# A passage between two projections, ordered by hand: from the output projection to gate/up in a two-layer trunk on one core

## The chip, the core and the metric

The kernel runs on one core of a Trainium2 chip, whose engines work side by side: TensorE (PE; its weight loads are shown apart as PEld), VectorE (DVE), ScalarE (ACT), GpSimd (POOL) and SyncE (SP), which issues most DMAs. The metric is the device time of one launch in microseconds (us), smaller is better; of several runs the median counts.

## What is computed

The reference is a trunk of two layers over 256 tokens of width 2048, all in float32. Around the change it does this:

```python
x = x + rms_norm(mix @ w_o, post_mix_norm[l])     # 2048 -> 2048
h = rms_norm(x, pre_ffn_norm[l])
f = (silu(h @ w_gate) * (h @ w_up)) @ w_down      # 2048 -> 5632 -> 2048
x = x + rms_norm(f, post_ffn_norm[l])
```

Here `mix` is the joined result of two kinds of attention. The passage meant by the change is the end of `mix @ w_o`, the norm and the sum into `x`, the transposition of the new `x`, and the first products with `w_gate` and `w_up`. It occurs once in each layer, so twice in a run.

## The kernel before

**Split products.** Every float32 product is made of three products of rounded numbers: a weight is split into a rounded part `hi` and a rest `lo`, the activations likewise into a rounded part and a rest, and PE adds hi x hi, hi x lo and lo x hi into one PSUM bank. A weight tile holds two blocks of 128 rows by 512 columns (128x1024 on the chip). ACT rounds it (L307, `hi`), DVE forms the rest (L317, `lo`). Some sums of a pair of weights are shared by Strassen's seven products (`seven_products`), which is not touched. In a few chosen places of gate/up the rest is made on GpSimd instead (L310).

**The stream of weights.** All weights lie in one list in the order of use. `fetch` issues their DMAs on SP ahead of time (four `raw` buffers), `feed` makes `hi` and `lo` (six buffers each) for the next one, and `weights(i, ahead)` feeds up to `ahead` further. Call the first of the last four `w_o` tiles `idx`: `idx`..`idx+3` are those four, `idx+4`/`idx+5` are gate and up for the first pair of blocks of x columns (pair 0), `idx+6`/`idx+7` for pair 1, `idx+8`/`idx+9` for pair 3, which comes third in the order of use, `idx+10`/`idx+11` for pair 2. A buffer of `hi` and `lo` comes free six weights later, so `idx+10` waits for the last use of `idx+4`.

**The tokens.** They form two tiles of 128, t0 and t1. The 2048 columns form four groups (cg0 to cg3) of 512, each with four blocks of 128.

**The end of the output projection.** Columns 2 and 3 of the projection are summed in four PSUM banks (two groups by two token tiles). The last four weights, 24 products for t0 and then 24 for t1, are issued so that t0 ends first. As each group ends, `evac_sum` adds the part shared by Strassen's products (L589), has ACT square it for the norm (L591 or L586) and multiplies by the gain (L592 or L587). `rescale` takes the root of the mean square: three small DVE operations (L599 to L601), Ln and Exp on ACT (L602, L603), one more on DVE (L604), a Newton step in two (L476, L477), and then four operations x = m * r + x, one per column group (L627).

**The transposition.** `transposed` turns one column group of x with four PE transposes into a bank of PSUM (tag `acc`, four banks), ACT rounds the four blocks with the next norm's gains (L488), and DVE makes the four rests (L493). The results are the stationary operands (`xF`) of gate/up.

**Gate/up.** `eight` (L1250) makes twelve products for one pair of blocks and one token tile. The first chunk takes pairs 0 and 1 for t0 and then for t1, and after them pairs 3, 2, 7 and so on for both tiles. Pairs 0 and 1 need cg0, pairs 3 and 2 need cg1, the others cg2 and cg3. The factor of the norm itself (`inv_rms`, eight squares L512 on ACT) is needed only at the end of a chunk.

**The order.** A list scheduler of the library fixes each engine's order ahead of the run, by priority (place in the program, or earlier by an offset under `high_priority`) and by its own estimate of when things are ready. Each engine then issues in that order and waits where an operand is late. In a `manual_schedule` region the named engines keep the order of the program among the region's instructions; where these fall among other instructions of that engine stays with the scheduler. Before the change such a region covers ACT and DVE from the last four `w_o` weights to the transposition of t0. The end of t1 (`evac_sum` of its last group, `rescale`, its transposes) stands outside under high priority.

Of the kernel before, what the change touches and what calls it, by code (L numbers as in the profile page):

```python
# [9 lines left out]
F32 = mybir.dt.float32  # L10
F32R = mybir.dt.float32r
BF16 = mybir.dt.bfloat16
AF = mybir.ActivationFunctionType
ALU = mybir.AluOpType
# [153 lines left out]
def kernel(  # L168
# [152 lines left out]

    rests = []
# [156 lines left out]

    def transposed(t, g0, tiles, cols=range(4)):  # L480
        for cg in cols:
            pb = acc_bank(f"xT_ps{t}_{cg}")
            for j in range(4):
                k = cg * 4 + j
                nc.tensor.transpose(pb[:, j * P : (j + 1) * P], x_part(t, k * P, P), ident)
            for j in range(4):
                k = cg * 4 + j
                rounded = nc.scalar.activation(  # L488
                    tiles[k][:, 0, t * P : (t + 1) * P], pb[:, j * P : (j + 1) * P], AF.Copy, scale=gains[:, g0 + k : g0 + k + 1]
                )  # L490
            for j in range(4):
                k = cg * 4 + j
                rest = nc.vector.scalar_tensor_tensor(  # L493
                    out=tiles[k][:, 1, t * P : (t + 1) * P],
                    in0=pb[:, j * P : (j + 1) * P],
                    scalar=gains[:, g0 + k : g0 + k + 1],
                    in1=tiles[k][:, 0, t * P : (t + 1) * P].bitcast(F32),
                    op0=ALU.mult,
                    op1=ALU.subtract,
                )  # L500
        return rounded, rest
# [4 lines left out]
    def inv_rms(t, pool, nm, parts=None):  # L506
        ss = small.tile([P, 1], F32, tag="ssx", name=f"ssx_{nm}_{t}")
        part = small.tile([P, 4], F32, tag="ssp", name=f"ssp_{nm}_{t}")
        for h in range(4):
            if parts is None:  # L510
                junk = pool.tile([P, CW], F32, tag="t2", name=f"junk_{nm}_{t}_{h}")
                nc.scalar.activation(junk, x_part(t, h * CW, CW), AF.Square, accum_out=part[:, h : h + 1])  # L512
            else:
                nc.scalar.activation(parts[h], parts[h], AF.Square, accum_out=part[:, h : h + 1])
# [66 lines left out]

    def evac_sum(pool, acc, mg, ssm, gpost, c, t, nm, summed=False):
        m = mg[t, c // 2][:, c % 2, :]
        if summed:
            junk = pool.tile([P, CW], F32, tag="t2", name=f"jm_{nm}_{t}_{c}")
            nc.scalar.activation(junk, acc, AF.Square, accum_out=ssm[t][:, c : c + 1])  # L586
            nc.vector.tensor_tensor(out=m, in0=acc, in1=gpost[:, c * CW : (c + 1) * CW], op=ALU.mult)  # L587
            return
        nc.vector.tensor_tensor(out=m, in0=acc, in1=m, op=shared_sign(t, c % 2))  # L589
        junk = pool.tile([P, CW], F32, tag="t2", name=f"jm_{nm}_{t}_{c}")  # L590
        nc.scalar.activation(junk, m, AF.Square, accum_out=ssm[t][:, c : c + 1])  # L591
        nc.vector.tensor_tensor(out=m, in0=m, in1=gpost[:, c * CW : (c + 1) * CW], op=ALU.mult)  # L592

    def rescale(mg, ssm, t, nm, then=None, newest=None):
        halves = newest is not None
# [5 lines left out]
        nc.vector.tensor_scalar(out=half, in0=three, scalar1=-0.5 / D, scalar2=-0.5 * EPS, op0=ALU.mult, op1=ALU.add)  # L601
        nc.scalar.activation(u, fourth, AF.Ln, scale=1.0 / D, bias=most)  # L602
        nc.scalar.activation(r, u, AF.Exp, scale=-0.5)  # L603
        nc.vector.tensor_scalar(out=ms, in0=fourth, scalar1=-0.5 / D, scalar2=half, op0=ALU.mult, op1=ALU.add)  # L604
        newton(r, u, ms)
        if halves:
# [8 lines left out]
        for c in range(4):  # L615
            if halves and c == 0:
                continue
            if halves and c == 3:
# [7 lines left out]
            sl = x_part(t, c * CW, CW)  # L626
            nc.vector.scalar_tensor_tensor(  # L627
                out=sl, in0=mg[t, c // 2][:, c % 2, :], scalar=r, in1=sl, op0=ALU.mult, op1=ALU.add
            )
# [505 lines left out]
    for l in range(L):  # L1135
# [48 lines left out]
        with tc.manual_schedule(engines={mybir.EngineType.Activation, mybir.EngineType.DVE}):  # L1184
            feed(idx + 6)
            for n, (c, kp) in enumerate(last_o):
                unit({0: accs[c, 0]}, mix, idx + n, kp, (0,), False, kp == LAST_O[-1], 0)
                if kp == LAST_O[-1]:
                    evac_sum(pool, accs[c, 0], mg, ssm, gpost, c, 0, f"o{l}")
            rescale(mg, ssm, 0, f"o{l}")  # L1190
            for n, (c, kp) in enumerate(last_o):
                feed(idx + 7 + n)
                fetch(min(idx + 12 + n, idx + 12))
                unit({1: accs[c, 1]}, mix, idx + n, kp, (1,), False, kp == LAST_O[-1], 0)
                transposed(0, 32 + l * KT, xT, cols=(n,))
                if (c, kp) == (2, LAST_O[-1]):
                    evac_sum(pool, accs[2, 1], mg, ssm, gpost, 2, 1, f"o{l}", True)
        with tc.high_priority(offset=URGENT):
            evac_sum(pool, accs[3, 1], mg, ssm, gpost, 3, 1, f"o{l}", True)
            rescale(mg, ssm, 1, f"o{l}", lambda t, c: transposed(t, 32 + l * KT, xT, cols=(c,)))  # L1200
        open_sums[0] = False
        rs = [inv_rms(t, pool, f"ffn{l}") for t in range(NT)]
# [272 lines left out]
```

## Time and profile before

| what | us |
|---|---|
| median of 3 runs | 2181.57 |
| lowest, highest | 2181.53, 2182.70 |
| profiled execution, whole | 2183.48 |
| its span, first to last instruction | 2181.7 |
| PE busy in the span | 2166.0 |
| DVE busy | 1920.7 |
| ACT busy | 1400.4 |
| POOL busy | 260.5 |

The profile is of one execution. Times in its views count from the start of the span. A row of the timeline gives the start, the duration, the engine, the line of the kernel, the operation, output and inputs, and how many like ones follow each other; in square brackets stands how long the engine was idle before and what released it. Products are pipelined: each is shown with 0.39 us, while the next starts after 0.23 us. In the view by windows each engine has its busy time and, in brackets, the number of its instructions.

### The profile page before, as it was taken

The numbers are of one execution on the slowest core, as the hardware profiler recorded it, in microseconds if no ns is written. First come the engines' busy times: TensorE is split into PE (matmuls) and PEld (weight loads), VectorE is DVE, ScalarE is ACT, GpSimd is POOL, SyncE is SP. The second block draws the span as 40 slices with busy tenths as digits, with TensorE's granted clock in tenths as the row PEclk, the third lists the DMA queues.
The fourth block names the chain that finished last, engine by engine and source line by source line (L and its number), as shares of the span: only waits on it lengthen the run. The fifth ranks groups of instructions, "written<-read, shape, count | busy, mean of one in ns | idle before, by whom it ended". The sixth has DMA issues, their size and how long they took to land.

```text
span 2181.7 us, 28784 instructions
## 1 busy us (share of the span) xinstructions
PE 2166.0 (99%) x9944; PEld 1781.7 (82%) x9944; DVE 1920.7 (88%) x2657; ACT 1400.4 (64%) x2089; POOL 260.5 (12%) x243
## 2 busy tenths in 40 slices
PE   9999999999999999999999999999999999999998
PEld 7888888788888888888878888887888888888886
DVE  7888658899999999999878886589999999999997
ACT  7666665756666656666665666657666666576664
POOL 1100000031222221000010000000212222200000
PEclk9999999999999999999999999999999999999999
DMA  9544555488887767767465555555888877768683
GB/s 323 194 164 174 193 184 176 165 300 234 239 258 229 226 231 233 239 223 258 149 241 174 172 174 188 191 164 191 286 237 241 262 222 227 240 225 244 204 268 100
DMA packets 140851, 471.49 MB, mean 216 GB/s; under 512 B 16016, under 2 KB 17040, under 8 KB 140192
## 3 DMA queue, kind: packets, MB, share of 16 engines
q1 hardware_dynamic: 121952, 436.03, 57.7%
q0 software_dynamic: 18176, 33.07, 9.2%
q8 instruction: 78, 1.28, 0.2%
q14 instruction: 69, 0.57, 0.1%
q10 hardware_dynamic: 576, 0.54, 0.1%
HBM read 461.19 MB, written 8.39 MB: 215 GB/s over the span
## 4 chain that ended last, share of the span: by engine, by line
PE 94%; DVE 3%; ACT 2%; issue 1%; DMA 0%; SPq 0%; DVEq 0%; ACTq 0%
PE c L1250 19%; PE in L1084 7%; PE in L1086 7%; PE in L1085 7%; PE dn L1357 4%; PE dn L1356 4%; PE dn L1359 4%; PE p L1085 3%; PE c L1084 3%; PE p L1084 3%; PE p L1086 3%; PE c L1085 3%; PE c L1086 3%; PE o L569 2%; PE o L571 2%; PE o L570 2%
## 5 line engine op out<-in xcount | busy, mean ns | idle before, releaser
L317 DVE TENSOR_TENSOR lo<-raw,hi 128x1024 fp32r<-128x1024 f32 x468 | 561.9, 1220 | 103.3 <-ACT hi L307 102.3
L307 ACT ACTIVATE hi<-raw 128x1024 fp32r<-128x1024 f32 x490 | 501.5, 1053 | 102.3 <-DMA raw<-in_weights_in_turn_dram 41.8
L1250 PE MATMUL c<-hi,xF 128*128 128x512 f32 x1280 | 345.9, 391 | 1.5 <-DVE xF L493 1.5
L1250 PEld LDWEIGHTS c<-hi,xF 128*128 128x128 f32 x1280 | 238.3, 188 | 50.3 <-DVE xF L493 2.0
L258 POOL DMA_DIRECT2D T<-in_weights_in_turn_dram x126 | 111.2, 883 | 1373.8 <-DMA T<-in_weights_in_turn_dram 716.6
L1250 PE MATMUL c<-lo,xF 128*128 128x512 f32 x640 | 198.2, 390 | 2.5 <-DVE lo L317 2.5
L279 ACT ACTIVATE Th<-G 128x1024 fp32r<-128x1024 f32 x126 | 133.1, 1056 | 79.8 <-DVE G L291 78.6
L281 DVE TENSOR_TENSOR Tl<-G,Th 128x1024 fp32r<-128x1024 f32 x126 | 153.9, 1221 | 10.1 <-ACT Th L279 10.1
L1356 PE MATMUL dn<-hi,jh 128*128 128x512 f32 x416 | 162.0, 389 | 0.0
L1357 PE MATMUL dn<-lo,jh 128*128 128x512 f32 x416 | 161.8, 389 | 0.0
L307 ACT ACTIVATE hi<-G 128x1024 fp32r<-128x1024 f32 x126 | 132.9, 1055 | 44.6 <-DMA G<-in_weights_in_turn_dram 27.8
L281 DVE TENSOR_TENSOR lo<-T,hi 128x1024 fp32r<-128x1024 f32 x126 | 159.6, 1266 | 0.3 <-ACT hi L279 0.2
L279 ACT ACTIVATE Th<-T 128x512 fp32r<-128x512 f32 x126 | 79.7, 633 | 118.6 <-DVE T L290 113.3
L291 DVE TENSOR_TENSOR G<-G,T 128x1024 f32<-128x1024 f32 x126 | 153.5, 1218 | 1.8
L1250 PEld LDWEIGHTS c<-lo,xF 128*128 128x128 f32 x640 | 120.1, 188 | 28.1 <-DVE lo L317 3.0
L317 DVE TENSOR_TENSOR lo<-G,hi 128x1024 fp32r<-128x1024 f32 x108 | 131.6, 1219 | 12.3 <-ACT hi L307 12.2
L279 ACT ACTIVATE hi<-T 128x1024 fp32r<-128x1024 f32 x126 | 132.2, 1049 | 12.1 <-PE c L1086 10.6
L1084 PE MATMUL in<-hi,xT 128*128 128x512 f32 x328 | 131.0, 401 | 0.6 <-DVE xT L862 0.6
L1084 PE MATMUL in<-hi,xI 128*128 128x512 f32 x328 | 131.1, 401 | 0.0
L1085 PE MATMUL in<-lo,xI 128*128 128x512 f32 x328 | 128.0, 390 | 0.3 <-DVE lo L317 0.3
L1085 PE MATMUL in<-lo,xT 128*128 128x512 f32 x328 | 127.8, 391 | 0.4 <-DVE lo L891 0.4
L1359 PE MATMUL dn<-hi,jl 128*128 128x512 f32 x416 | 128.0, 389 | 0.0
(485 smaller groups left out, 4954.2 us busy)
## 6 DMA issues: line engine op xcount, KB each, us to landing
raw<-in_weights_in_turn_dram SPq DMA_DIRECT2D x490, 512.0 KB, 4.6
T<-in_weights_in_turn_dram SPq DMA_DIRECT2D x126, 512.0 KB, 5.3
G<-in_weights_in_turn_dram SPq DMA_DIRECT2D x126, 512.0 KB, 5.4
T<-in_weights_in_turn_dram POOLq DMA_DIRECT2D x126, 256.0 KB, 6.1
GU<-in_weights_in_turn_dram SPq DMA_DIRECT2D x32, 512.0 KB, 6.5
V<-in_weights_in_turn_dram SPq DMA_DIRECT2D x8, 512.0 KB, 3.7
away_ffn<-x SPq DMA_DIRECT2D x8, 512.0 KB, 8.2
xd<-away_ffn SPq DMA_DIRECT2D x8, 512.0 KB, 9.4
```

Source lines behind the costliest of these rows:

```text
L279: nc.scalar.activation(h, w, AF.Copy)
L281: newest_rest[i] = nc.vector.tensor_tensor(out=l, in0=w, in1=h.bitcast(F32), op=ALU.subtract)
L291: nc.vector.tensor_tensor(out=g, in0=g, in1=t2.unsqueeze(1).to_broadcast([P, 2, CW]), op=ALU.add)
L307: nc.scalar.activation(hi, raw, AF.Copy)
L317: rest = nc.vector.tensor_tensor(out=lo, in0=raw, in1=hi.bitcast(F32), op=ALU.subtract)
L1084: nc.tensor.matmul(a, sh, hi, start=first, stop=False, skip_group_check=open_sums[0])
L1085: nc.tensor.matmul(a, sh, lo, start=False, stop=False, skip_group_check=open_sums[0])
L1086: return nc.tensor.matmul(a, sl, hi, start=False, stop=last, skip_group_check=open_sums[0])
L1250: nc.tensor.matmul(a, stat[part], w[j][:, kk, :], start=first and kk + n == 0, stop=last and kk == 1 and n == 2)
L1356: nc.tensor.matmul(accs[c, t], sh, hi[:, kk, :], start=first, stop=False, skip_group_check=open_sums[0])
L1357: nc.tensor.matmul(accs[c, t], sh, lo[:, kk, :], start=False, stop=False, skip_group_check=open_sums[0])
L1359: nc.tensor.matmul(accs[c, t], sl, hi[:, kk, :], start=False, stop=last, skip_group_check=open_sums[0])
```

## The change

One region now covers ACT, DVE and PE from the last four `w_o` weights on, and a second one, under high priority, covers ACT and DVE for the rest of the passage.

- `idx+5` is split behind the square of t0's group 2, and not ahead of the sum that this square reads.
- All 48 last products of the output projection stand ahead of t0's sixteen transposes on PE; all four groups of t0 are turned at once into the four `acc` banks.
- Of t0 only cg0 and cg1 are rounded and get rests before t1's turn; cg2 and cg3 come behind t1's cg0 and cg1.
- The rest of `idx+7` (up, pair 1) is made on GpSimd, behind the rest of `idx+6`, to which it has a dependence.
- The root for t1 is interleaved by hand with the splits of `idx+8` and `idx+9`, the gains of t1's groups 2 and 3 come behind the first two sums into x.
- The eight squares of `inv_rms` are issued on ACT behind the rounding of t1's cg0 (`turned`).

The same functions are cut into smaller ones (`turned_x`, `rounded_x`, `rest_of_x`, `squared`, `gained`, `shared_added`, `root_of`, `rescaled`); the operations in them are the same. `rounded_next` issues the rounding of the next weight and gives back a function that makes its rest. The core of the diff:

```diff
+    def rounded_next():
+        i = fed[0]
+        fetch(i + 1)
+        raw = raws[i]
+        hi = wpool.tile([P, 2, CW], F32R, tag="hi", bufs=6, name=f"hi{i}")
+        nc.scalar.activation(hi, raw, AF.Copy)
+        lo = wpool.tile([P, 2, CW], F32R, tag="lo", bufs=6, name=f"lo{i}")
...
+        def rest(eng=nc.vector):
+            r = eng.tensor_tensor(out=lo, in0=raw, in1=hi.bitcast(F32), op=ALU.subtract)
...
-        with tc.manual_schedule(engines={mybir.EngineType.Activation, mybir.EngineType.DVE}):
-            feed(idx + 6)
+        by_hand = {mybir.EngineType.Activation, mybir.EngineType.DVE}
+        with tc.manual_schedule(engines=by_hand | {mybir.EngineType.PE}):
+            feed(idx + 5)
             for n, (c, kp) in enumerate(last_o):
                 unit({0: accs[c, 0]}, mix, idx + n, kp, (0,), False, kp == LAST_O[-1], 0)
-                if kp == LAST_O[-1]:
-                    evac_sum(pool, accs[c, 0], mg, ssm, gpost, c, 0, f"o{l}")
-            rescale(mg, ssm, 0, f"o{l}")
+                if n == 1:
+                    squared(pool, shared_added(accs[2, 0], mg, 2, 0), ssm, 2, 0, nm)
+                    feed(idx + 6)
+            gained(mg[0, 1][:, 0, :], mg, gpost, 2, 0)
+            squared(pool, shared_added(accs[3, 0], mg, 3, 0), ssm, 3, 0, nm)
+            gained(mg[0, 1][:, 1, :], mg, gpost, 3, 0)
+            rescale(mg, ssm, 0, nm)
+            rest_a = rounded_next()
+            fetch(idx + 12)
             for n, (c, kp) in enumerate(last_o):
-                feed(idx + 7 + n)
-                fetch(min(idx + 12 + n, idx + 12))
                 unit({1: accs[c, 1]}, mix, idx + n, kp, (1,), False, kp == LAST_O[-1], 0)
-                transposed(0, 32 + l * KT, xT, cols=(n,))
-                if (c, kp) == (2, LAST_O[-1]):
-                    evac_sum(pool, accs[2, 1], mg, ssm, gpost, 2, 1, f"o{l}", True)
-        with tc.high_priority(offset=URGENT):
-            evac_sum(pool, accs[3, 1], mg, ssm, gpost, 3, 1, f"o{l}", True)
-            rescale(mg, ssm, 1, f"o{l}", lambda t, c: transposed(t, 32 + l * KT, xT, cols=(c,)))
+            squared(pool, accs[2, 1], ssm, 2, 1, nm)
+            pb = [turned_x(0, cg) for cg in range(4)]
+            rounded_x(pb[0], 0, 0, g0, xT)
+            rest_of_x(pb[0], 0, 0, g0, xT, (0, 1))
+            rest_a = rest_a()
+            rest_of_x(pb[0], 0, 0, g0, xT, (2, 3))
+            rest_b = rounded_next()(nc.gpsimd)
+            tc.add_manual_dep(rest_b.ins, rest_a.ins.name, AFTER, reason="the shared port")
+            rounded_x(pb[1], 0, 1, g0, xT)
+            squared(pool, accs[3, 1], ssm, 3, 1, nm)
+            root = root_of(ssm, 1, nm)
+            next(root)
+            rest_c = rounded_next()
+            next(root)
+            rest_of_x(pb[1], 0, 1, g0, xT)
+            rest_c()
+            r = next(root)
+            rounded_next()()
+        with tc.manual_schedule(engines=by_hand), tc.high_priority(offset=URGENT):
+            rescaled(mg, 1, 0, r)
+            pb += [turned_x(1, 0)]
+            rescaled(mg, 1, 1, r)
+            pb += [turned_x(1, 1)]
+            gained(accs[2, 1], mg, gpost, 2, 1)
+            gained(accs[3, 1], mg, gpost, 3, 1)
+            turned = rounded_x(pb[4], 1, 0, g0, xT)
+            rest_of_x(pb[4], 1, 0, g0, xT)
+            rounded_x(pb[5], 1, 1, g0, xT)
+            rescaled(mg, 1, 2, r)
+            rescaled(mg, 1, 3, r)
+            rest_of_x(pb[5], 1, 1, g0, xT)
+            for cg in (2, 3):
+                rounded_x(pb[cg], 0, cg, g0, xT)
+                rest_of_x(pb[cg], 0, cg, g0, xT)
+            transposed(1, g0, xT, cols=(2, 3))
         open_sums[0] = False
-        rs = [inv_rms(t, pool, f"ffn{l}") for t in range(NT)]
+        rs = [inv_rms(t, pool, f"ffn{l}", behind=turned) for t in range(NT)]
```

In `root_of` the three `yield`s stand behind L601, behind L604 and behind the Newton step, so that other work can be put between these parts.

## The prediction on record

> **What bounds the kernel now.** The page comes first.
>
> ```profile
> span 2181.7 us, 28784 instructions
> PE 2166.0 (99%) x9944; PEld 1781.7 (82%) x9944; DVE 1920.7 (88%) x2657; ACT 1400.4 (64%) x2089; POOL 260.5 (12%) x243
> ```
>
> PE is busy 99% of the span, so only time in which PE waits can be won. The view of waits, for PE alone, says for what it waits; these two of its nine rows lie where the change is, four waits, two in each layer:
>
> ```profile
> PE c L1250 <- DVE lo L317: 2.5, 2, 1.3
> PE c L1250 <- DVE xF L493: 1.5, 2, 0.7
> ```
>
> The timeline of PE and PEld places them. The first rows are layer 0, the windows below them layer 0 and then layer 1.
>
> ```profile
> 392.57 0.39 PE L570 MATMUL o<-lo,mix_df 128*128 128x512 f32 x1
> 393.04 1.32 PE L485 MATMUL xT_ps<-ident,x 128*128 128x128 f32 x8
> 394.11 0.48 PE L571 MATMUL o<-hi,mix_df 128*128 128x512 f32 x1
> 396.42 1.19 PE L1250 MATMUL c<-hi,xF 128*128 128x512 f32 x4 [0.74 <-DVE xF L493]
> 397.45 0.61 PE L1250 MATMUL c<-lo,xF 128*128 128x512 f32 x2
> 397.90 1.07 PE L1250 MATMUL c<-hi,xF 128*128 128x512 f32 x4
> 398.81 0.61 PE L1250 MATMUL c<-lo,xF 128*128 128x512 f32 x2
> 403.64 1.08 PEld L485 LDWEIGHTS xT_ps<-ident,x 128*128 128x128 f32 x8
> 403.80 1.16 PE L485 MATMUL xT_ps<-ident,x 128*128 128x128 f32 x8
> 406.21 0.50 PE L1250 MATMUL c<-lo,xF 128*128 128x512 f32 x1 [1.25 <-DVE lo L317]
> ...
> 392.80:396.42 3.62, 2.79 (x18) 1.84 (x17) 3.62 (x7) 2.69 (x8) 0.00 (x0) 1.00 0.02 5
> 403.80:406.21 2.41, 1.16 (x9) 0.78 (x8) 2.41 (x6) 2.41 (x12) 0.00 (x0) 1.00 0.60 212
> 1478.77:1482.39 3.62, 2.79 (x19) 1.84 (x18) 3.62 (x7) 2.69 (x8) 0.00 (x0) 1.00 0.00 0
> 1489.83:1492.17 2.34, 1.09 (x10) 0.78 (x8) 2.34 (x6) 2.34 (x11) 0.00 (x0) 1.00 0.53 205
> ```
>
> Products start 0.227 us apart (four from 397.90 to 398.81), eight transposes take 1.08 (their weight loads). From 392.80, when the product after that of 392.57 was due, to the first gate product at 396.42 go 3.62 us; in them are one product (0.23) and sixteen transposes (2.16), so **1.23 is lost**, waiting for t0's x, its rounding and its rests. Four products from 396.42 take 1.03 and not 0.91: 0.12 lost. From 403.80 to 406.21 go 2.41 for eight transposes: **1.33 lost**, for a weight's rest. Layer 1 has the same windows (3.62 and 2.34). That is 2.7 us a layer, 5.3 in all, 0.25% of the time. No more can be had here, and that is about what a measurement tells from no change (0.2%, 4.4 us, is my bound for "same").
>
> Why PE waits shows in DVE's and ACT's rows of the same stretch:
>
> ```profile
> 384.38 1.06 ACT L307 ACTIVATE hi<-raw 128x1024 fp32r<-128x1024 f32 x1 [0.32 <-PE o L571]
> 384.10 1.23 DVE L317 TENSOR_TENSOR lo<-raw,hi 128x1024 fp32r<-128x1024 f32 x1 [2.35 <-ACT hi L307]
> 386.62 0.68 DVE L589 TENSOR_TENSOR mg_o<-o,mg_o 128x512 f32<-128x512 f32 x1
> 387.34 0.63 ACT L591 ACTIVATE jm_o<-mg_o 128x512 f32<-128x512 f32 x1 [1.89 <-DVE mg_o L589]
> 388.10 0.69 DVE L592 TENSOR_TENSOR mg_o<-mg_o,gpost_mix 128x512 f32<-128x512 f32 x1 [0.79 <-ACT jm_o L591]
> 388.70 0.68 DVE L589 TENSOR_TENSOR mg_o<-o,mg_o 128x512 f32<-128x512 f32 x1
> 390.18 0.69 DVE L592 TENSOR_TENSOR mg_o<-mg_o,gpost_mix 128x512 f32<-128x512 f32 x1 [0.79 <-ACT jm_o L591]
> 391.78 0.22 DVE L476 SCALAR_TENSOR_TENSOR tot_o<-tot_o 128x1 f32<-128x1 f32 x1 [0.35 <-ACT tot_o L603]
> 392.23 2.74 DVE L627 SCALAR_TENSOR_TENSOR x<-mg_o,tot_o,x 128x512 f32<-128x512 f32 x4
> 393.73 1.14 ACT L488 ACTIVATE xF<-xT_ps,gains 128x128 fp32r<-128x128 f32 x4 [1.03 <-PE xT_ps L485]
> 394.89 1.22 DVE L317 TENSOR_TENSOR lo<-raw,hi 128x1024 fp32r<-128x1024 f32 x1
> 396.02 1.12 DVE L493 SCALAR_TENSOR_TENSOR xF<-xT_ps,gains,xF 128x128 fp32r<-128x128 f32 x4
> 397.06 1.21 DVE L317 TENSOR_TENSOR lo<-raw,hi 128x1024 fp32r<-128x1024 f32 x1
> 404.94 1.22 DVE L317 TENSOR_TENSOR lo<-raw,hi 128x1024 fp32r<-128x1024 f32 x1
> 406.07 2.15 DVE L493 SCALAR_TENSOR_TENSOR xF<-xT_ps,gains,xF 128x128 fp32r<-128x128 f32 x8
> ```
>
> In the windows DVE is busy to the last hundredth (3.62 of 3.62, 2.41 of 2.41). At 404.94 it makes the rest of idx+9, which PE's next product reads; t1's first rests come at 406.07. Before them it has made all sixteen rests of t0, of which eight (cg2, cg3) are not needed for another twenty products or more.
>
> **The change, part by part.**
>
> *The sums of t0 (first wait).* idx+4's rest ends at 384.10 + 1.23 = 385.33; t0's group 2 is ready about 385.0, so its sum now starts at 385.25 in place of 386.62. Its square ends (by the step from 386.62 to 387.34, plus 0.73 to 388.07) at 386.7. But idx+5's rounding now stands behind this square on ACT (before: 384.38): 386.55 to 387.6, and its rest stands ahead of the gain on DVE: 387.65 to 388.8. The gain starts at 388.75 (before 388.10), the sum of group 3 at 389.35 (before 388.70), everything to the x sums 0.65 later: L627 starts at 392.9 and not at 392.23. DVE idles 1.8 us ahead of idx+5's rest, which costs nothing itself, but this step **loses 0.65** on the chain to x.
>
> *All products ahead of the transposes.* PE now reaches t0's transposes at 393.03 with nothing left behind. They follow x by 0.81 (392.23 to 393.04); L627 advances by 0.665 (four from 392.23 to 394.89), so the fourth starts at 394.9, its transposes at 395.7, and they end at 396.25. The first rests stand behind the fourth L627 at 395.55 and no longer behind a weight's rest (before: 394.89, rests at 396.02); the first ends at 395.9. The gate starts at **396.25 in place of 396.42**, bound by the fourth group of transposes, which it doesn't need. Won: 0.17, and the 0.12, since both weights and two rests are there.
>
> *DVE from there to t1's first rest (second wait).* Pitches from the rows above: a weight's rest 1.13, four rests of x 1.04, a gain 0.6 (388.10 to 388.70), the Newton step 0.45 (391.78 to 392.23), and as much for the four small operations ahead of Ln and Exp. Two rests of x to 396.1, idx+6 to 397.2, two rests to 397.75, small ones to 398.25, cg1 to 399.3, idx+8 to 400.4, Newton to 400.9, two sums into x to 402.2, two gains to 403.4, first rest of t1 at **403.8**; with idx+9 ahead of them, which the scheduler may choose, 404.9. Before it was 406.4. What left this stretch: idx+7's rest (1.13) and eight rests of x (2.08). ACT keeps ahead of it: transposes at 393.7, rounding from 394.4 (0.69 behind, as 393.73 stands to 393.04), then about 1.0 each for cg0, idx+7 and cg1, 0.7 for t1's last square, 1.0 for idx+8 and 0.6 for Ln and Exp, which end near 399.7, with idx+9 behind them.
>
> ```profile
> 402.00 0.76 ACT L512 ACTIVATE junk_ffn<-x 128x512 f32<-128x512 f32 x1
> 411.57 0.89 POOL L258 DMA_DIRECT2D T<-in_weights_in_turn_dram  x1 [261.72 <-DMA T<-in_weights_in_turn_dram]
> L310 POOL TENSOR_TENSOR lo<-raw,hi x22: 2400/2444/3155, 438.7 to 1895.3; 128x1024 fp32r<-128x1024 f32 x22
> 444.01 2.99 POOL L310 TENSOR_TENSOR lo<-raw,hi 128x1024 fp32r<-128x1024 f32 x1 [1.43 <-ACT hi L307]
> 446.45 0.70 DVE L1091 TENSOR_TENSOR s<-f 128x128 f32<-128x128 f32 x1
> 447.07 0.28 DVE L1093 TENSOR_TENSOR s<-f 128x128 f32<-128x128 f32 x1
> ```
>
> PE meanwhile: 24 products from 396.25 to 401.7, twelve of pair 3 (ten without idx+9's rest) and eight transposes of t1: it runs dry at 405.05 with ten (401.7 + 2.27 + 1.08), 405.5 with twelve. So t1's rests come 0.6 to 1.2 us before PE needs them, and the wait of 1.33 should go. Against errors in this long sum I leave 0.2 a layer.
>
> *idx+7 on GpSimd.* A rest takes 2.40 to 3.16 there, the median 2.44: from 397.25 to 399.7 or 400.4; PE needs it at the eighteenth product, 396.25 + 17 x 0.227 = 400.1. So 0 to 0.3; I take 0. DVE is relieved of 1.13. The queue behind it on POOL holds only the accumulating DMA for the first summed weight, which in layer 0 starts at 411.6: nobody waits. The buffer of idx+7 comes free 1.5 later for idx+11, needed near 410: covered.
> Two rows show what the two engines do to each other: the DVE operation at 446.45 takes 0.70, the next of its shape 0.28, and ends where GpSimd's ends (444.01 + 2.99). A DVE operation on two SBUF operands that meets idx+7's rest can so be held until 399.7: the rest of idx+8, by 0.4 at most, which the slack of 0.6 holds. [...]
>
> *The squares of inv_rms.* Four of the eight squares, 0.76 each, stood from 402.00 ahead of t1's rounding on ACT. They move behind it. ACT is not late for t1 in my sum (transposes at 401.7, rounding from 402.4, by DVE's 403.4), so this only keeps ACT out of the way; undone, it would cost up to 3.0. Behind `turned`, ACT still has the rounding of four groups and idx+10, idx+11, not due before t1 is through pair 0, twelve products after 405: 408. Free.
>
> *cg2, cg3 of t0 late.* Needed by pair 7, after pairs 0, 1, 3, 2 for both tiles (96 products, 21.8 us from 396.25). Free.
>
> *DMAs.* The same loads in the same order; `fetch(idx + 12)` asks for no more than before. idx+9's buffer comes free 2.1 later (388.8 for 386.7), eleven us ahead of its rounding at 399.7: covered.
>
> Sum for a layer: 0.17 + 0.12 + 1.33 - 0.2 = 1.42; for two **2.9 us**. The profiled execution (2183.48 whole, span 2181.7) would come to 2180.6; it lies 1.9 above the median 2181.57 of the runs, from which I forecast **2178.7**.
>
> **The rivals.**
>
> *The wait only moves.* DVE stays the bound: idx+9 ahead of t1, GpSimd at its 3.16 and the holding of 0.4 add up to more than the slack, and PE waits for idx+7's rest or t1's. For it: DVE without a gap in the windows. Against it: 3.2 us less work for it. Only 0.3 a layer is won: 2181.0 (2179.8 to 2182.5).
>
> *Both waits go.* If the x sums don't slip by 0.65, but come as much earlier as the sum of group 2 does, PE's first wait falls by 0.9 more at most: 2 x 2.3 to 2.65, 2176.3 to 2177. Against it: idx+5's rest stands between two links of this chain.
>
> *Slower: idx+9's rest falls behind the second region.* The last instruction of the first region and the high priority of the second compete on DVE; everything of the second that is ready goes first. Behind t1's cg0 (404.9), the two last x sums (406.2), t1's cg1 (407.2) and t0's cg2 and cg3 (409.3) idx+9 ends at 410.5. If PE's fixed order has its products ahead of t1's, PE waits from 405.05 to 410.5, 5.45 for 1.33: 2 x (4.1 - 0.3) = 7.6 slower, 2189.2. It decides from 406.7 on (no gain), each us later costs two. Against it: the scheduler would have to misjudge DVE by that much, and it set PE's order before so that it fell short by 1.3.
>
> *Nothing done*: the two regions change the order of three engines for certain; I give this no chance of its own.
>
> **How the numbers follow.** Forecast 52%, wait moves 21%, both go 11%, slower 16%. The forecast's own range is 2177.3 to 2180.3. Range over all: from the whole loss won, 2176.2, to 2185.5, half way to the slower rival's time, which leaves its worse half and little else out. Faster by over 0.2% (under 2177.2) are the third case and a small end of the first: 0.14. Slower by over 0.2% (above 2185.9) is most of the fourth: 0.13. Same: 0.73.
>
> **What would show it.** In the PE timeline of layer 0: sixteen transposes in one stretch from about 393.7; first gate product near 396.25; no gap over 0.3 between 401 and 407. In DVE's: L627 of t0 at 392.9 (right) or earlier (both waits go); L493 of t1 before 405; idx+9's rest before 406. In POOL's: one L310 near 397.3 that ends by 400.1. Wrong I am if t0's L627 starts before 392.2, if PE waits over 1 us for t1 or a weight's rest after 400, or if a wait appears anywhere after 415, where there is none now.

## The result, and the profile after

| what | us |
|---|---|
| changed kernel, median of 10 runs | 2187.41 (2186.05 to 2188.43) |
| kernel before, beside it, median of 10 runs | 2181.68 (2180.95 to 2182.71) |
| ratio | 1.0025, 95% interval 1.0016 to 1.0035 |
| profiled execution after, whole | 2186.9 |
| its span | 2185.2 |

The change makes the kernel slower, by 5.7 us where 2.9 less was forecast. The time lies above the range. The first two lines of the page after and, of the view of PE's waits, three rows that before did not have (the last is the wait for t0's x ahead of its transposes):

```profile
span 2185.2 us, 28773 instructions
PE 2168.2 (99%) x9944; PEld 1780.8 (81%) x9944; DVE 1920.8 (88%) x2655; ACT 1398.3 (64%) x2089; POOL 266.3 (12%) x245
...
PE c L1327 <- ACT hi L307: 3.4, 2, 1.7
...
PE p L1127 <- DVE Tl L281: 1.2, 2, 0.8
PE xT_ps L502 <- DVE x L646: 1.2, 2, 0.6
```

The two rows of before, 2.5 us for a weight's rest and 1.5 for t0's first rests of x, are gone. In their place PE waits twice, 1.7 us each, for a rounding by ACT. The timeline of PE after, layer 0, shows where (the output projection's last product, the sixteen transposes of t0, which are called flips from here on, the first gate products, those behind t1's first flips, and pair 2):

```profile
392.29 0.39 PE L600 MATMUL o<-hi,mix_df 128*128 128x512 f32 x1
393.26 2.64 PE L502 MATMUL xT_ps<-ident,x 128*128 128x128 f32 x16 [0.58 <-DVE x L646]
395.65 1.17 PE L1327 MATMUL c<-hi,xF 128*128 128x512 f32 x4
405.10 1.19 PE L1327 MATMUL c<-hi,xF 128*128 128x512 f32 x4
413.88 0.61 PE L1327 MATMUL c<-lo,xF 128*128 128x512 f32 x2
416.20 1.77 PE L1327 MATMUL c<-hi,xF 128*128 128x512 f32 x6 [1.71 <-ACT hi L307]
```

This execution runs 0.51 us ahead of the one before: its last output product starts at 392.29, so the next would be due at 392.52, where the same place was due at 392.80 + 0.23 = 393.03 by before's rows. With 0.51 added, the first gate product is at 396.16 (before 396.42), and the gap of 1.33 before t1's products is 0.18 (404.92 to 405.10, two products behind 404.46). The new gap is at the end: the product after 413.88 and its twin is due at 414.33 and comes at 416.20, **1.87 us late**. It is the first of pair 2, the fourth pair in the order 0, 1, 3, 2, 7, and reads `idx+10`. A wait after 415, where before had none, is one of the signs by which the prediction said that it would be wrong. The timeline of ACT after says why; with it the two rows of before to hold beside it, `idx+10`'s rounding and t0's third square:

```profile
403.52 4.54 ACT L508 ACTIVATE xF<-xT_ps,gains 128x128 fp32r<-128x128 f32 x17 [3.56 <-PE xT_ps L502]
407.96 0.62 ACT L541 ACTIVATE junk_ffn<-x 128x512 f32<-128x512 f32 x1
408.57 0.36 ACT L508 ACTIVATE xF<-xT_ps,gains 128x128 fp32r<-128x128 f32 x1
413.78 0.64 ACT L541 ACTIVATE junk_ffn<-x 128x512 f32<-128x512 f32 x1
415.08 1.07 ACT L307 ACTIVATE hi<-raw 128x1024 fp32r<-128x1024 f32 x1
```

```profile
403.23 0.75 ACT L512 ACTIVATE junk_ffn<-x 128x512 f32<-128x512 f32 x1
409.04 1.06 ACT L307 ACTIVATE hi<-raw 128x1024 fp32r<-128x1024 f32 x1 [1.07 <-PE c L1250]
```

ACT stood idle for 3.56 us up to 403.52, waiting for t1's first flip. In that stretch before made t0's four squares (402.00 to 404.46). After, ACT then makes seventeen roundings, and from 407.96 on eight squares with the last seven roundings between them. Only at 415.08 comes `idx+10`, which before had at 409.04. Its product follows 1.12 later. DVE, whose queue holds the small sums of these squares, gets behind too, as the views by windows of after and of before show (DVE's busy time is the fourth number):

```profile
380.00:427.00 47.00, 44.67 (x207) 35.31 (x206) 38.53 (x90) 32.23 (x81) 4.17 (x3) 1.00 0.56 185
```

```profile
380.00:427.00 47.00, 44.92 (x209) 36.24 (x209) 40.80 (x96) 33.39 (x82) 1.76 (x2) 1.00 0.55 188
```

Of the 2.3 us less, 1.2 is `idx+7`'s rest, which GpSimd makes; the other 1.1 is work that DVE has not yet done by then.

For the rest of the document the lost time of PE is set against before place by place. From PE's timeline, 0.227 us for each product issued and 0.135 for each flip are taken from the time that passed; the rest is lost, and what before lost up to the same place is subtracted. "Passage" is up to 412 us (1500 in layer 1), "pair 2" up to 430 (1520), "gate/up" up to 856 (1980); each includes what lies ahead. The first column is the median less that of before on the same chip.

| kernel | median | passage | pair 2 | gate/up | passage, layer 1 | pair 2 | gate/up |
|---|---|---|---|---|---|---|---|
| after | +5.7 | -1.44 | +0.59 | +2.28 | -1.45 | +0.69 | +1.66 |
| after, second profile (h2) | | -1.45 | +0.58 | +2.34 | -1.45 | +2.25 | +3.12 |
| e1, squares free | -1.7 | -1.42 | -1.52 | -1.75 | -1.49 | -1.38 | -0.13 |
| e1, second profile (h3) | | -1.43 | -1.54 | -0.73 | -1.50 | -1.31 | -0.97 |
| f2, four squares late | -0.5 | -1.41 | -1.46 | -0.49 | -1.48 | -1.37 | -1.13 |
| e2, squares behind pair 2 | -1.0 | -1.48 | -1.60 | -0.77 | -1.42 | -1.13 | -0.59 |
| e3, rest of idx+7 on DVE | +4.9 | -0.57 | +1.36 | +1.61 | -0.64 | +1.65 | +2.27 |
| e4, before with squares late | +0.4 | +0.02 | +0.32 | -0.89 | -0.03 | +0.35 | +0.40 |
| f1, e1 with an earlier flip | -3.2 | -1.63 | -1.77 | -2.98 | -1.68 | -1.65 | -3.14 |
| h1, after with an earlier flip | +2.4 | -1.98 | +0.02 | -0.30 | -2.02 | +0.10 | +0.69 |

The first two columns of each layer repeat within 0.1 where a kernel has two profiles, apart from one cell, which is told of below; the third differs by up to a microsecond. The profile of before that is subtracted belongs to an execution 1.9 us above the median, so the third columns read too well by as much, over both layers. With the edges of the windows set a little otherwise, the third columns shift by up to 0.3.

### The profile page after: what moved, and what is told of

Read it like the earlier page. It is cut to its first block, busy times and chain, and to the rows that moved or that the text cites. A ratio compares the mean times of both kernels' runs of the same rounds, so it can differ in the third digit from the quotient of the medians.

```text
span 2185.2 us, 28773 instructions
## 1 busy us (share of the span) xinstructions
PE 2168.2 (99%) x9944; PEld 1780.8 (81%) x9944; DVE 1920.8 (88%) x2655; ACT 1398.3 (64%) x2089; POOL 266.3 (12%) x245
## 4 chain that ended last, share of the span: by engine, by line
PE 86%; DVE 7%; ACT 3%; issue 2%; DMA 2%; SPq 0%; DVEq 0%; ACTq 0%
PE c L1327 17%; PE in L1126 6%; PE in L1128 6%; PE in L1127 6%; PE dn L1436 4%; PE dn L1434 4%; PE dn L1433 4%; PE p L1127 3%; PE c L1127 2%; PE c L1126 2%; PE p L1128 2%; PE c L1128 2%; PE p L1126 2%; PE o L598 2%; PE o L600 2%
## 5 line engine op out<-in xcount | busy, mean ns | idle before, releaser
L317 DVE TENSOR_TENSOR lo<-raw,hi 128x1024 fp32r<-128x1024 f32 x460 | 553.0, 1224 | 109.6 <-ACT hi L307 108.6
L307 ACT ACTIVATE hi<-raw 128x1024 fp32r<-128x1024 f32 x482 | 492.1, 1052 | 106.4 <-DMA raw<-in_weights_in_turn_dram 48.4
L1126 PE MATMUL in<-hi,xI 128*128 128x512 f32 x328 | 131.1, 401 | 0.0
L1128 PE MATMUL in<-hi,xI 128*128 128x512 f32 x328 | 128.0, 391 | 0.0
```

The source lines that it names most:

```text
L307: nc.scalar.activation(hi, raw, AF.Copy)
L317: rest = nc.vector.tensor_tensor(out=lo, in0=raw, in1=hi.bitcast(F32), op=ALU.subtract)
L1126: nc.tensor.matmul(a, sh, hi, start=first, stop=False, skip_group_check=open_sums[0])
L1128: return nc.tensor.matmul(a, sl, hi, start=False, stop=last, skip_group_check=open_sums[0])
```

## The experiments

The theory from the traces: the passage won what was forecast, and the eight squares, put behind t1's first rounding, hold up `idx+10` on ACT, so that PE gives it back at pair 2. The rivals were GpSimd's rest, another effect of the new order, and DVE as the pace of what follows.

**e1: the squares free.**

```diff
-        rs = [inv_rms(t, pool, f"ffn{l}", behind=turned) for t in range(NT)]
+        rs = [inv_rms(t, pool, f"ffn{l}") for t in range(NT)]
```

> The changed kernel, but inv_rms's eight squares may stand anywhere on ACT again, not behind the rounding of t1's first columns. Theory A (the squares, moved out of ACT's idle stretch, stand ahead of the rounding of idx+10 and make PE wait at pair 2, and DVE's idle time there is paid later in the chunks): in this order five squares stand in the idle stretch near 400 to 403, three ahead of idx+10, which is rounded near 411 and not 415; PE's wait of 1.9 us there falls under 0.5, and the whole is 2178 to 2180.5. Theory B (GpSimd's rest or the new order as such makes the later waits): the direct wait goes, what is lost later stays: 2183 to 2184.5.

Measured: 2180.41 against 2182.12 of before, ratio 0.9995 (0.9986 to 1.0004). Theory A. Two rows of ACT and the first product of pair 2 in e1:

```profile
404.77 5.31 ACT L508 ACTIVATE xF<-xT_ps,gains 128x128 fp32r<-128x128 f32 x20
412.79 1.10 ACT L307 ACTIVATE hi<-raw 128x1024 fp32r<-128x1024 f32 x1
415.58 1.30 PE L1327 MATMUL c<-hi,xF 128*128 128x512 f32 x5
```

`idx+10`'s rounding starts at 412.79 and PE doesn't wait for it. This execution runs 1.26 us behind the changed kernel's (last output product at 393.55 against 392.29), so t1's rounding begins at the same place as there, 403.51 against 403.52: the five squares that stand ahead of it again cost nothing here. One line is worth over 7 us of the changed kernel (+5.7 against -1.7). Whether the time is below before's can't be told.

**e2: the squares emitted within chunk 0, ahead of the third of its later pairs.**

```diff
-        rs = [inv_rms(t, pool, f"ffn{l}", behind=turned) for t in range(NT)]
...
             for n, kp in enumerate(order):
+                if c == 0 and n == 2:
+                    rs = [inv_rms(t, pool, f"ffn{l}") for t in range(NT)]
```

> The changed kernel, but inv_rms is emitted inside the first chunk, behind the feeding for pair 3, so that idx+10 and idx+11 come ahead of all eight squares on ACT. Theory A: idx+10 is rounded near 409, no wait at pair 2, the gain of the passage (about 2 us a layer) is kept: 2176.5 to 2179, faster than before. Theory B: 2183 to 2184.5.

Measured: 2181.12, ratio 0.9995 (0.9986 to 1.0004): between the two. `idx+10`'s rounding in e2:

```profile
409.63 1.07 ACT L307 ACTIVATE hi<-raw 128x1024 fp32r<-128x1024 f32 x1
```

It starts earlier than in any other kernel of the changed family, there is no wait at pair 2, and the squares come even later than in the change (from 421.25 on). So it isn't that the squares are late, but what they stand ahead of. That `idx+10` came some 3 us earlier than in e1 won nothing more.

**e3: the rest of idx+7 on DVE.**

```diff
-            rest_b = rounded_next()(nc.gpsimd)
-            tc.add_manual_dep(rest_b.ins, rest_a.ins.name, AFTER, reason="the shared port")
+            rounded_next()()
```

> The changed kernel with the rest of idx+7 on DVE in place of GpSimd, all else as changed. Theory A: the wait at pair 2 stays as it is, t1's first rests come up to 1.1 us later: 2187 to 2189. Theory B, if GpSimd's lock is what costs: 2183 to 2185.

Measured: 2186.98, ratio 1.0022 (1.0014 to 1.0031): as the changed kernel, just under the lower edge of theory A's range, and theory B falls. What that theory calls GpSimd's lock stands in the rows as a longer rest on DVE beside one on GpSimd: 1.62 for `idx+8` in the changed kernel, while the four weights' rests that begin between 395.9 and 401.9 in e3 take 1.22 or 1.23. In the passage the rest on GpSimd is worth 0.8 to 0.9 us a layer by the table (-0.57 against -1.44), since without it PE waits again for t1's rests; these are the timeline's rows of PE in e3:

```profile
406.22 1.19 PE L1326 MATMUL c<-hi,xF 128*128 128x512 f32 x4 [0.95 <-DVE xF L516]
417.26 1.79 PE L1326 MATMUL c<-hi,xF 128*128 128x512 f32 x6 [1.62 <-ACT hi L307]
```

The wait for ACT is there as well. What the passage lost more doesn't show in the whole time.

**e4: the kernel before, with its squares behind the rounding of t1's cg0.** `transposed` there gives back the last rounding, which `inv_rms` takes as `behind`.

```diff
-            rescale(mg, ssm, 1, f"o{l}", lambda t, c: transposed(t, 32 + l * KT, xT, cols=(c,)))
+            turned = []
+            rescale(mg, ssm, 1, f"o{l}", lambda t, c: turned.append(transposed(t, 32 + l * KT, xT, cols=(c,))[0]))
...
-        rs = [inv_rms(t, pool, f"ffn{l}") for t in range(NT)]
+        rs = [inv_rms(t, pool, f"ffn{l}", behind=turned[0]) for t in range(NT)]
```

> The kernel before with this one part of the change alone: the eight squares are issued on ACT behind the rounding of t1's first columns. Theory A: idx+10 is rounded near 415 in place of 409, PE waits 1 to 2 us a layer at pair 2 and as much again is paid later: 2184.5 to 2187.5. Theory B: within 1 us of before, 2181 to 2182.5.

Measured: 2182.55, ratio 1.0003 (0.9994 to 1.0012): theory B, the part alone costs nothing that can be told. The rounding of `idx+10` and the first products of pair 2 in e4:

```profile
413.49 1.14 ACT L307 ACTIVATE hi<-raw 128x1024 fp32r<-128x1024 f32 x1
416.03 1.07 PE L1252 MATMUL c<-hi,xF 128*128 128x512 f32 x4
416.94 0.93 PE L1252 MATMUL c<-lo,xF 128*128 128x512 f32 x2
```

The rounding starts some 4.8 us later than in before (at 413.49, in an execution that runs 0.35 ahead). But PE, which still loses its two waits in the passage, comes to pair 2 only at 416.03, when the rounding is done, and loses no more than 0.3 us there, for a rest. Before's own waits had hidden it: the squares' place costs only once the passage is shorter.

**f2: four of the eight squares late, those of t1.**

```diff
-        rs = [inv_rms(t, pool, f"ffn{l}", behind=turned) for t in range(NT)]
+        rs = [inv_rms(t, pool, f"ffn{l}", behind=turned if t else None) for t in range(NT)]
```

> The changed kernel with only the second tokens' four squares behind the flipped columns; the first tokens' four are free. Theory A (the price is the length of ACT's queue ahead of idx+10's rounding, which ends at 416.0 in the changed kernel and must end by about 414.3): four squares fewer, 4 x 0.83 us, put idx+10's rounding at about 412, no wait of PE at the second pair, time as e1, 2179.5 to 2182. Theory B (the cause is another effect of the line, for instance the late square sums that DVE's queue waits for, or the changed list order later on, and half of the late squares keep half of it): 2183 to 2185.5.

Measured: 2180.90 against 2181.36, ratio 0.9998 (0.9989 to 1.0007): theory A. ACT's timeline in f2:

```profile
403.40 5.32 ACT L508 ACTIVATE xF<-xT_ps,gains 128x128 fp32r<-128x128 f32 x20 [1.27 <-PE xT_ps L502]
408.60 0.64 ACT L541 ACTIVATE junk_ffn<-x 128x512 f32<-128x512 f32 x1
412.33 1.09 ACT L307 ACTIVATE hi<-raw 128x1024 fp32r<-128x1024 f32 x1
```

The other four squares stand in the idle stretch again (1.27 left of 3.56), `idx+10` begins at 412.33 and PE runs through pair 2. Four squares out of the queue moved it by 415.08 - 412.33 = 2.75, less 0.13 by which this execution runs ahead of the other: 0.65 each, and not the 0.83 of the expectation. By the changed kernel's rows it may begin up to 414.33 - 1.12 = 413.2: four fit, eight miss it by 1.9.

**f1: e1, and t0's chain to x shortened.** `idx+5`'s rest no longer stands between the sums of groups 2 and 3, and the last gain stands behind the first part of x.

```diff
                 if n == 1:
                     squared(pool, shared_added(accs[2, 0], mg, 2, 0), ssm, 2, 0, nm)
-                    feed(idx + 6)
+                    rest_5 = rounded_next()
             gained(mg[0, 1][:, 0, :], mg, gpost, 2, 0)
             squared(pool, shared_added(accs[3, 0], mg, 3, 0), ssm, 3, 0, nm)
-            gained(mg[0, 1][:, 1, :], mg, gpost, 3, 0)
-            rescale(mg, ssm, 0, nm)
+            root = root_of(ssm, 0, nm)
+            next(root)
+            rest_5()
+            next(root)
+            r = next(root)
+            for c in range(4):
+                if c == 1:
+                    gained(mg[0, 1][:, 1, :], mg, gpost, 3, 0)
+                rescaled(mg, 0, c, r)
```

> The changed kernel with the squares of inv_rms free (as e1) and, besides, the chain to x of the first 128 tokens shortened: idx+5's rest goes behind the addition of column 3 and the three small sums, and the last multiplication by the gain behind the first flipped part. From the changed kernel's rows the root then starts about 1.1 us earlier and the flips of the first tokens no longer wait (0.74 us lost there in both of the last kernels). Theory A (what PE wins in the passage stays until PE meets an engine that is as late, and DVE, 97% busy in the chunks, takes part of it back): passage gain 2.1 to 2.2 us a layer instead of 1.45 at 430 us, whole time 2178.5 to 2181, at most 1 us below e1. Theory B (what is won in the passage is worth its full size in the whole time): 1.4 us below e1, 2177.5 to 2179.5.

Measured: **2178.14** (2176.82 to 2179.94) against 2181.36, ratio 0.9986 (0.9977 to 0.9995): faster than before by 0.14%, and so than the changed kernel. The time is theory B's: 2.3 us below e1 by the medians, 1.5 by the differences to before. Neither had the passage right. Rows of PE, DVE and ACT in f1:

```profile
392.54 1.91 PE L502 MATMUL xT_ps<-ident,x 128*128 128x128 f32 x16
390.11 0.75 DVE L646 SCALAR_TENSOR_TENSOR x<-mg_o,tot_o,x 128x512 f32<-128x512 f32 x1
404.93 1.19 PE L1334 MATMUL c<-hi,xF 128*128 128x512 f32 x4 [0.59 <-DVE xF L516]
403.36 5.29 ACT L508 ACTIVATE xF<-xT_ps,gains 128x128 fp32r<-128x128 f32 x20
```

The first part of x starts at 390.11 instead of 392.45, and the flips follow the last output product without a wait. But 0.6 us of a wait for t1's rests is back (404.93), so the passage wins only 0.2 a layer more than e1's and not 0.6 to 0.7. The rest of the gain lies behind it, where single executions differ by a microsecond; why it is kept there is not shown.

**h1: the changed kernel, its squares where the change puts them, with f1's shorter chain.** The edit is the one shown for f1, without e1's line.

> The changed kernel, squares behind the flipped columns as in the change, with only the chain to x of the first tokens shortened as in f1 (there it made the whole time some 2 us less than e1, and PE won 0.6 us a layer more in the passage). Theory A (in the changed kernel the second pair starts when ACT comes to idx+10's rounding, whenever PE gets there; what PE wins ahead of it is lost in the wait): rounding of idx+10 at about 415 to 416 as before the edit, the wait of TensorE at the second pair 0.3 to 0.7 us longer than in the changed kernel, whole time 2186 to 2188. Theory B (the won time adds up whatever the ACT queue does): 2183.5 to 2186.

Measured: 2184.38 against 2181.97, ratio 1.0011 (1.0002 to 1.0020): theory B, and theory A falls in the form given. PE and ACT in h1, behind t1's first flip and at pair 2:

```profile
403.74 4.56 ACT L508 ACTIVATE xF<-xT_ps,gains 128x128 fp32r<-128x128 f32 x17 [3.82 <-PE xT_ps L502]
405.32 1.21 PE L1334 MATMUL c<-hi,xF 128*128 128x512 f32 x4 [0.25 <-DVE xF L516]
416.44 1.77 PE L1334 MATMUL c<-hi,xF 128*128 128x512 f32 x6 [1.70 <-ACT hi L307]
415.32 1.07 ACT L307 ACTIVATE hi<-raw 128x1024 fp32r<-128x1024 f32 x1
```

PE's wait is the same 1.70, not longer. ACT's queue is no fixed clock: it starts with t1's first flip, and that comes earlier when t0's chain does. This execution runs 0.76 us behind the changed kernel's (last output product at 393.05), so t1's rounding begins 0.54 earlier in it (403.74 against 403.52). What PE wins ahead of the flip moves both. In these two kernels pair 2 costs some 2 us whatever stands ahead of the flip: from the first rounding behind it to the product that `idx+10` releases pass 416.20 - 403.52 = 12.7 us, and PE has work for 414.33 - 403.52 = 10.8.

The passage wins more here than in f1 (-1.98 against -1.63), although the edit on t0's chain is the same (the 0.6 over e1 that the expectation gives to f1 was 0.2). In f1 two of the free squares, at 402.07 and 402.73, hold ACT until t1's rounding at 403.36, 0.99 behind the first flip of t1 (402.37). In h1 the rounding follows the flip by 0.64 (403.10 and 403.74), and the wait for t1's rests is 0.25 instead of 0.59. So with the shorter chain the squares have a price of 0.35 ahead of t1's rounding too. Squares behind `idx+10`, as in e2, together with f1's chain were not run.

**f3 and f4: DVE relieved.** In before (f3) and in e1 (f4) two rests a chunk are left out: where PE would read `lo` it reads `hi` again, so these two kernels do the same number of products but don't compute the reference's result.

```diff
+    spared = {lay["up"][c, kp] for lay in plan for c in range(1, FF // CW) for kp in (0, 7)}
...
+            if i in spared:
+                ready[i] = (hi, hi)
+                fed[0] += 1
+                continue
```

> The kernel before, with the rests of two up weights (column groups 0 and 7) left out in every chunk but the first: TensorE multiplies by the rounded weight twice, as many products as before, and DVE has about 2 x 1.22 us less in each chunk of some 41 us, 97% busy there before. Control for the next kernel. If DVE sets the pace of the chunks: the 3.2 us that TensorE loses between 420 and 860 us in layer 0 (and 2.5 in layer 1) go for the most part, 2175 to 2179. If not: within 1 us of before.

> The changed kernel with the squares free (as e1) and the same rests left out as in the control. Read against the control: theory A (of the 1.45 us a layer that the passage wins, the chunks take a part back because DVE, nearly full, is what PE catches up with): with DVE relieved the distance to the control is the whole passage gain, 2.5 to 3.2 us. Theory B (the part is given back for another reason, the order of the instructions further on, or DMA): the distance stays at that of e1 to before, 0.7 to 2 us.

Measured: 2197.22 (2194.64 to 2197.92) and 2196.22 (2193.77 to 2198.24) against 2181.36. Both are some 15 us slower with less work, which no theory allowed, and the 1.0 us between them is less than their spread. The largest waits of PE in f3 and in f4 are of a kind for which PE never waits in before:

```profile
PE c L1255 <- ACT act L1235: 9.9, 12, 2.3
PE c L1332 <- ACT act L1312: 7.7, 13, 1.9
```

They are 9.9 of the 16 us in f3 and 7.7 of the 15 in f4. What PE waits for are ACT's copies of the transposed activations out of PSUM, which free banks that later products write. With less work on DVE the scheduler also gave ACT another order, all through the chunks, in f3 than in before and in f4 than in e1. That the copies come late for this reason is likely, not shown, and the rest of the 15 us was not traced. So the pair can't say whether DVE takes back what the passage wins, and that stays open.

**h2 and h3: the changed kernel and e1, each profiled once more.**

> The changed kernel once more, for a second profile. In its first profile TensorE loses 1.4 us more than before between 422 and 540 us and 0.94 us at one place near 598, where a rest on DVE had taken 2.38 us instead of 1.22 beside a rest on GpSimd. Theory A (this stands in the order of the instructions, so that a full DVE is met every time): the same rest takes 2 us or more again and TensorE loses within 0.5 us of 1.4 between 422 and 840 again. Theory B (where the two rests meet changes from run to run): that rest takes 1.2 to 1.5 us and another one is long, or none.

> The changed kernel with the squares free (e1) once more, for a second profile: how far the lost time by place differs between two executions of one kernel. In the first the passage wins 1.4 to 1.5 us on before in both layers, and the rest of gate and up gives back 0.4 us less than nothing in layer 0 (1.8 us won at 840) and 1.3 us in layer 1. Theory A (the passage's gain is fixed, and what follows differs by a microsecond or more from run to run): 1.3 to 1.6 us in both passages, and other numbers behind them. Theory B (the give-back belongs to the kernel): within 0.3 us of the first profile at both ends.

Measured: 2188.20 and 2181.20, one run each. The passage and pair 2 of layer 0 repeat within 0.02 us for the changed kernel. For it, theory A holds in layer 0: the same rest on DVE is long again, and PE waits at the same place. DVE, GpSimd and PE in the first profile, then DVE and PE in the second:

```profile
575.23 2.38 DVE L317 TENSOR_TENSOR lo<-raw,hi 128x1024 fp32r<-128x1024 f32 x1
573.78 2.73 POOL L310 TENSOR_TENSOR lo<-raw,hi 128x1024 fp32r<-128x1024 f32 x1
598.28 0.50 PE L1127 MATMUL p<-Tl,sh 128*128 128x512 f32 x1 [0.76 <-DVE Tl L281]
```

```profile
575.14 2.48 DVE L317 TENSOR_TENSOR lo<-raw,hi 128x1024 fp32r<-128x1024 f32 x1
598.50 0.50 PE L1127 MATMUL p<-Tl,sh 128*128 128x512 f32 x1 [0.77 <-DVE Tl L281]
```

In e1 the same rest took 1.23 in the first profile and 1.6 in the second (1.21 in h1), and PE doesn't wait there. Against e1's first profile DVE stands 0.87 us later where this rest begins (575.23 against 574.36), 2.02 later at its next instruction, and still 1.8 later at the rest `Tl` that PE waits for (597.00 against 595.19), while PE itself stands 0.43 later just ahead of it; so the delay of the long rest reaches PE. GpSimd's rest of 573.78 ends at 576.5, and the DVE rest that begins at 575.23 ends 1.1 behind it, about its own length; in the second profile the two end 1.1 apart as well (576.5 and 577.6), and in before, where the rest took 1.47, too (574.3 and 575.4). For e1, theory A holds: 1.4 to 1.5 won in both passages, and behind them up to a microsecond of difference between two executions.

## Why the prediction failed

*The sums of t0, right.* L646 (L627 in before) starts at 392.45 + 0.51 = 392.96, forecast 392.9. The 0.65 that the step loses shows as the wait of 0.74 which PE still has before the flips; in f1, where this rest is out of the chain and the last gain moved as well, it is gone.

*All products first, right.* The gate starts at 396.16 on before's clock, forecast 396.25. The 0.12 of the sum did not come: the first four products take 1.02 (395.65 to 396.67) where they took 1.03, although nothing is late. It was no wait; the first product behind a stretch of flips takes 0.32 there, and 0.34 in before.

*DVE to t1's first rest, right in effect.* The rows of DVE and GpSimd after:

```profile
397.10 2.41 POOL L334 TENSOR_TENSOR lo<-raw,hi 128x1024 fp32r<-128x1024 f32 x1 [247.73 <-DVE lo L334]
398.97 1.62 DVE L334 TENSOR_TENSOR lo<-raw,hi 128x1024 fp32r<-128x1024 f32 x1
400.86 1.22 DVE L334 TENSOR_TENSOR lo<-raw,hi 128x1024 fp32r<-128x1024 f32 x1
404.70 1.13 DVE L516 SCALAR_TENSOR_TENSOR xF<-xT_ps,gains,xF 128x128 fp32r<-128x128 f32 x4
```

The scheduler put `idx+9`'s rest first, so t1's rests stand at 405.21 on before's clock (forecast 404.9 for that case), and 0.18 of the 0.2 left for errors was used. That is later than the "before 405" which the prediction named as a sign of being right. The slower rival, with this rest behind the second region, didn't come.

*idx+7 on GpSimd, right.* 2.41, and `idx+8`'s rest was held by 0.4 (1.62 for 1.22; GpSimd's ends at 399.51, this one 1.08 behind it), as was said. By e3 it is worth 0.8 to 0.9 a layer in the passage.

The passage so won 1.44 and 1.45 us, where 1.42 was forecast. That it agrees to 0.03 is partly luck: the gate gave 0.26 for 0.17, the 0.12 gave nothing.

*The squares: the step that failed.* "Behind `turned`, ACT still has the rounding of four groups and idx+10, idx+11, not due before t1 is through pair 0, twelve products after 405: 408. Free." No sum stood behind this word, and it left out the squares themselves. With the prediction's own durations it would have been: t1's rounding from 402.4, six groups of 1.0 and eight squares at the step of 0.61 (402.00 to 402.62) to 413.3, some 0.4 for two roots, `idx+10` to 414.8. PE comes to pair 2 after 72 products and sixteen flips, 396.25 + 16.3 + 2.2 = 414.8. So nothing was left to spare even in the better of its two cases; in the other one, with `idx+9`'s rest first, which it named itself (404.9 for 403.8) and which came, 1.1 us a layer were missing. The groups that it counted behind `turned` are also five and not four. Measured on the same clock, the rounding began not at 402.4 but at 404.03, since DVE made `idx+9`'s rest ahead of t1's x, and `idx+10` let PE go at 416.7 where PE was due at 414.8: the 1.87. The due time of 408 was also wrong, and on the safe side. Undoing the step (e1) or half of it (f2) takes the loss away; done alone in before (e4) it costs nothing that can be told. So this step is shown to be the one that failed. Its other price, "undone, it would cost up to 3.0", was wrong too: undone, in e1, it cost nothing in the passage (-1.42 and -1.49 against -1.44 and -1.45).

*Behind the passage, unpriced.* The prediction had no term after pair 2. From -1.44 the changed kernel goes to +0.59 there, in layer 1 from -1.45 to +0.69: the passage wins 2.9, pair 2 costs 4.2, and together they are 1.3 us of the 5.7. The other 4.4 or so are lost further on: 1.7 and 1.0 in the profile, and up to 1.9 by which the profile of before lies above its median. Of the 7.4 us between the changed kernel and e1, 4.2 are so at pair 2; the other 3.2 go with the same line, but behind it, and how is for the most part open. One collision of DVE and GpSimd, with 0.94 us of PE by the reckoning of the table, is shown, in both profiles; it is absent in h1, e1 and e3, whose order of instructions on DVE, ACT and GpSimd differs from the changed kernel's only in the passage; why the two rests meet in the one and not in the others is not shown. That a DVE which is 1.1 us behind can't catch up in chunks where it is 96% busy (327.15 of 340 us from 460 to 800 in before), and so explains the rest, was argued, not shown: f3 and f4 were to try it and couldn't. In e1, e2 and f2 the same columns take back 1.2 to 2.3 us of the 2.7 to 2.9 won up to pair 2, by the medians, each uncertain by about 2.

*The late groups cg2, cg3, and the DMAs* cost nothing that a row shows.

## What to carry over

A step "moved to where there is room" needs the same sum as a step on the path: all that stands in that engine's queue from the event that starts it, the moved work included, against the time at which the next user is due in the new schedule, not in the old one. A wait that is taken away shortens the cover of everything behind it, and work which fits in the idle stretch of an engine ahead of an event (here 3.56 us of ACT) lengthens the queue by its full length behind that event, and what is over the cover is paid. Where a scheduler lays out the rest, an edit that takes work away can cost more than the work (some 15 us in f3 and f4), so the relief of an engine is not a clean experiment.

## What the runs showed of the hardware

Behind one of the eight long waits at pair 2 in the profiles of after, h2, e3 and h1 stands a second loss. In the second profile of the changed kernel the wait of layer 1 is as long as elsewhere, but the products behind it come 0.42 us apart for a while. The view by windows of that execution, whose column ahead of the last two is the clock that TensorE was granted:

```profile
1502.00:1504.20 2.20, 0.52 (x4) 0.10 (x2) 1.44 (x6) 2.20 (x8) 0.00 (x0) 1.00 0.29 51
1504.20:1506.20 2.00, 2.00 (x7) 1.45 (x8) 1.95 (x4) 2.00 (x4) 0.00 (x0) 0.88 0.02 4
1506.20:1510.00 3.80, 3.80 (x12) 2.99 (x11) 3.80 (x7) 2.75 (x3) 0.00 (x0) 0.61 0.79 247
1510.00:1514.00 4.00, 4.00 (x20) 3.29 (x19) 4.00 (x8) 2.95 (x4) 0.00 (x0) 1.00 0.77 294
```

For 3.8 us it was 0.61, twelve products started there instead of seventeen, and this is the cell of the table that doesn't repeat: 1.6 us more. Ahead of it PE had started no product for 2.06 us (1502.11 to 1504.17; the next was due at 1502.33, so it was 1.84 late). In the first profile of the changed kernel it started none for 2.09 us in layer 0 (414.11 to 416.20) and for 2.06 in layer 1 (1502.27 to 1504.33), and the clock behind both is 1.00 in the views by windows. So the clock fell behind one such wait in eight; what made the one differ from the seven is not shown.
